# The second gate of a hybrid block as pairs of seven half-depth products, with the compressed tokens and both gates in another order

## The chip, the cores and the metric

The kernel runs on 1 core of one Trainium2 chip. The metric is the device time of one execution in microseconds. The kernel before takes 1617.92 us, the median of 3 runs (1616.51 to 1618.95).

## What is computed

One decoder block for a sequence of 1024 positions of width 1024. Two branches read the same normalized input `xn`: a gated linear recurrence (branch a) and a sparse attention over compressed, selected and window tokens (branch b). A sigmoid gate per channel weighs each branch before they are added:

```python
proj = xn @ w_in[l]
a_q, a_f, a_i, a_g, b_q, b_kv, b_gate, m_gate = jnp.split(proj, SPLIT_POINTS, axis=-1)
kc, vc, ks_, vs_, kw_, vw_ = jnp.split(b_kv, 6, axis=-1)
y_a = hgrn2_mixer(a_q, a_f, a_i, a_g, lb_all[l], hgrn_norm_g[l])
y_b = nsa_mixer(b_q, kc, vc, ks_, vs_, kw_, vw_, b_gate, positions, ...)
g_a, g_b = jnp.split(jax.nn.sigmoid(m_gate), 2, axis=-1)
merged = g_a * (y_a @ w_br_a[l]) + g_b * (y_b @ w_br_b[l])
h = h + merged @ w_out[l]
hn = rmsnorm(h, norm2_g[l])
h = h + jnp.square(jax.nn.relu(hn @ w_ff1[l])) @ w_ff2[l]
```

`m_gate` is 2048 wide: 1024 columns for the gate of branch a, 1024 for that of branch b. In `nsa_mixer` a small network (`compress`) makes 63 compressed keys and values per group out of `kc` and `vc`.

## The kernel before, in words

All matrix products run on TensorE on split numbers: each float32 operand is a high part and a remainder, and a product is three matmuls (`mm3`, L248 to L252: high by high, high by low, low by high). A matmul here has 128 rows of weights and 512 columns. x is kept transposed in `XT[th][q]`, where `th` is one half of the positions and `q` one half of the 1024 input channels, each as a pair `xh`, `xl`.

Weights come through a stream, `W` (L124 to L165): SP loads a tile `wraw`, ScalarE casts it to the high part `whi` (L152), and the remainder `wlo` is a subtraction (L155), on VectorE for two tiles of three and on GpSimd for the third. `get` starts loads and splits some tiles ahead. A second stream `C` (L658) brings the weights of `compress`.

The part that matters here runs, before the change, in this order:

1. Queries, forget gates and values of branch a, with the heads of the recurrence in the background.
2. The first gate and branch a's output, in the order of the list `ZSEQ`: m0 m1 m2 z0 m3 z1 ... m7 z5 z6 z7. An m is one tile of 128 gate columns over all positions (`gemm_T`, 48 matmuls, into PSUM tile `gT`) with a sigmoid of three ScalarE passes (L296 to L298). A z is one tile of `y_a @ w_br_a` (24 matmuls, into `pz`); VectorE multiplies it by the gate (L621), and SP stores it to DRAM (`ma_d`). Two z share one weight tile.
3. The compressed tokens: eight products `pp` (L631 to L638).
4. The second gate: eight more tiles of `gemm_T` with sigmoid, stored to `gb_d` (L750 to L754). `compress` (L663 to L746) runs beside them, first for keys, then for values: its hidden layer is `ph`, four chunks of 12 matmuls of 256 columns (L706 to L708), each with one weight tile of `C` and one operand `fh` that ScalarE (L699) and VectorE (L700) make in 8 instructions each; then a gelu on VectorE (L713 to L720) and two small products (`pgl`, `pc`).
5. Branch b's projections, `proj_b(0)`, then attention, merge, output product, MLP. The first stage of the MLP (`f1a` to `f1d`) already works in pairs of tiles with seven products each.

Background work is Python generators: `spawn` starts one, `pump` (called inside the products) gives it a step when its own program time has come, `drain` runs it to its end at that place of the program. The tile framework then fixes one order of instructions for each engine, and each engine works its own list strictly in that order.

Below, `ph` chunk means 12 matmuls of the hidden layer. "m6" and "z4" name tiles as above. The functions are printed with the line numbers of the profile.

Of the kernel before, what the change touches and what calls it, by code (L numbers as in the profile page):

```python
# [33 lines left out]
C_AQ, C_AF, C_AI, C_AG, C_BQ, C_KV, C_BG, C_MG = 0, 512, 1024, 1536, 2048, 2560, 3328, 3352  # L34


def split_const(v, bits=12):
    parts = []
    r = v
    for _ in range(3):  # L40
        e = math.floor(math.log2(abs(r)))
        s = 2.0 ** (e - bits + 1)
        p = math.floor(r / s) * s
        parts.append(p)
        r -= p
# [9 lines left out]
def tile_hybrid_block(ctx, tc, x, positions, norm1_g, w_in, lb_param, hgrn_norm_g, pe_k, pe_v,  # L55
                      w1_k, w2_k, w1_v, w2_v, w_br_a, w_br_b, w_out, norm2_g, w_ff1, w_ff2,
                      final_g, out):
    nc = tc.nc
# [5 lines left out]
    dram = ctx.enter_context(tc.tile_pool(name="dram", bufs=1, space=bass.MemoryType.DRAM))  # L64
# [4 lines left out]
    w_in2 = w_in[0]  # L69

    def psA(name="psA"):
        return ps.tile([128, 1024], F32, name=name, tag="A", bufs=2)

    def psB(name="psB"):
        return ps.tile([128, 512], F32, name=name, tag="B", bufs=4)

    def s4(dt=F32, name="s4"):
        return sl4.tile([128, 1024], dt, name=name, tag="s4", bufs=NS4)

    def a8(name="a8"):  # L80
        return act.tile([128, 4, 512], F32R, name=name, tag="a8", bufs=8)


    bg = []
    clock = [0.0]

    def pump(ns):
        clock[0] += ns
        for e in list(bg):
            while e[1] <= clock[0]:  # L90
                try:
                    lag = next(e[0])
                except StopIteration:
                    bg.remove(e)
                    break
                e[1] = clock[0] + lag

    def spawn(gen, delay=0.0):
        e = [gen, clock[0] + delay]
        bg.append(e)  # L100
        return e

    def drain(e):
        while e in bg:
# [19 lines left out]
    class Stream:  # L124
# [5 lines left out]
        def add(self, srcs, shape):  # L130
            self.specs.append((srcs if isinstance(srcs, list) else [srcs], shape))
# [60 lines left out]
    def add_vg2(h):  # L192
        for i in range(4):
            W.add([vg_w[:, i * 2:(i + 1) * 2, e, h * 128:(h + 2) * 128] for e in range(2)], (2, 512))

    for h in range(1, 4):
# [3 lines left out]
            add_vg(h)  # L200
        elif h == 2:
            add_vg2(h)
    ZSEQ = []
    for ct in range(8):
        ZSEQ.append(("m", ct))
        if ct >= 2:
            ZSEQ.append(("z", ct - 2))
    ZSEQ += [("z", 6), ("z", 7)]
    for kind, ct in ZSEQ:
        if kind == "m":  # L210
            add_mg(ct)
        elif ct % 2 == 0:
            W.add(w_cols(w_br_a[0], ct * 128, 256, k=4), (4, 256))
    for k0, k in ((0, 3), (3, 3), (6, 2)):
        W.add([w_cols(w_in2, C_KV, 256, k0=k0, k=k), w_cols(w_in2, C_BG, 24, k0=k0, k=k)], (k, 280))
    for ct in range(8):
        add_mg(8 + ct)
# [67 lines left out]
    def gemm_T(w, o=None):  # L285
        o = o or psA("gT")
        for th in range(2):
            for kt in range(KT):
                mm3(o[:, th * 512:(th + 1) * 512], (w[0][:, kt, :], w[1][:, kt, :]), X_mov(kt, th),
                    kt == 0, kt == KT - 1)  # L290
                if kt % 4 == 3:
                    pump(2600)
        return o

    def sigmoid(dst, src, tmp):
        nc.scalar.activation(tmp, src, AF.Exp, scale=-1.0)  # L296
        nc.scalar.activation(tmp, tmp, AF.Ln, bias=1.0)
        nc.scalar.activation(dst, tmp, AF.Exp, scale=-1.0)  # L298
# [3 lines left out]
    yaT = {}  # L302
# [105 lines left out]
    P1, P2, P3, P4 = split_const(2.0 * math.pi)  # L408
# [4 lines left out]
    for which in range(2):  # L413
# [7 lines left out]
        r = trig[:, which]  # L421
# [157 lines left out]
    hg = [spawn(hgrn(0))]  # L579
# [45 lines left out]
    cos, sin = trig[:, 0], trig[:, 1]
    gat = attc.tile([128, NT, 24], F32)
# [3 lines left out]
    kct = [s4(name="kct").rearrange("p (t c) -> p t c", t=4) for _ in range(2)]  # L630
    for t in range(NT):  # L631
        p = psB("pp")
# [130 lines left out]
    def proj_b(th):  # L763
        for dst, n in ((KV, "kvt"), (QT, "qt")):
            ws = [W.get() for _ in range(4)]
            dst[th] = [s4(name=n).rearrange("p (t c) -> p t c", t=2) for _ in range(2)]
            for j in range(4):
                p = psB("pp")
                for kt in range(KT):
                    w = ws[kt // 2]  # L770
                    mm3(p, X_st(kt, th * 4 + j), (w[0][:, kt % 2, :], w[1][:, kt % 2, :]), kt == 0, kt == KT - 1)
                    if kt % 2 and kt < 7:
                        pump(1300)
                nc.scalar.copy(dst[th][j // 2][:, j % 2, :], p)
# [644 lines left out]
    for th in range(2):  # L1419
# [11 lines left out]
        for dh in range(2):  # L1431
# [54 lines left out]
    for s, (k, a, b) in enumerate(seq):  # L1486
# [6 lines left out]
        i, p = a, b  # L1493
# [50 lines left out]
```

## Time and profile before

| | |
|---|---|
| median of 3 runs | 1617.92 us (1616.51 to 1618.95) |
| the profiled execution's own time | 1621.0 us |
| its span in the profile | 1619.0 us |
| mean granted clock of TensorE | 0.997 |
| TensorE (PE) busy | 1597.3 us, 99% of the span |
| VectorE (DVE) busy | 1090.5 us, 67% |
| ScalarE (ACT) busy | 744.7 us, 46% |
| GpSimd (POOL) busy | 579.8 us, 36% |

The profiled execution took 3.1 us more than the median of the runs. The span ends 2.0 us short of its execution's own time. The engine names in the rows are PE for matmuls, PEld for loads of weights into TensorE, DVE, ACT, POOL, and SP for the queue that issues the transfers. The share of busy time is a mean over stages with different limits; the change touches the stretch from about 262 us (end of the recurrence) to about 525 us (first projection of branch b).

### The profile page before, as it was taken

The page shows a single profiled execution, that of the slowest core. Times are in us where ns is not written, and L with a number is a line of the kernel's source. Part 1 is how long each engine was busy: PE and PEld are TensorE (multiplying, and loading weights), DVE is VectorE, ACT ScalarE, POOL GpSimd, SP SyncE. Part 2 cuts the span into 40 slices and gives each one's busy share as a digit, 9 for nine tenths or more (in the row PEclk, how much of TensorE's full clock was granted, in tenths as well). Part 3 has the DMA queues.
Part 4 walks back from the last instruction along what each step waited for, and adds up shares of the span by engine and source line. Part 5 has one row for each costly group of instructions (what it writes and reads, how often), then busy time and mean ns, then how long its engine had stood idle before and what let it go on. Part 6 is the DMA issues. An engine that isn't in the chain of part 4 may idle for free.

```text
span 1619.0 us, 22567 instructions
## 1 busy us (share of the span) xinstructions
PE 1597.3 (99%) x8150; PEld 1331.3 (82%) x8150; DVE 1090.5 (67%) x1635; ACT 744.7 (46%) x1430; POOL 579.8 (36%) x567
## 2 busy tenths in 40 slices
PE   8999999999999999999999999999999999999998
PEld 7898888889888888788878887888888888888886
DVE  5554444122537466988887567888999868888766
ACT  4344244230646365877774324433333445334443
POOL 2122122010112364434341124455665302654454
PEclk9999999999999999999999999999999999999999
DMA  6201011232425000000028742344444599988752
GB/s 190 73 27 53 21 45 27 89 109 79 134 91 172 27 1 1 1 1 1 1 66 286 264 139 78 134 153 144 150 143 152 205 345 315 324 302 312 281 187 104
DMA packets 143777, 211.64 MB, mean 131 GB/s; under 512 B 11649, under 2 KB 70193, under 8 KB 143666
## 3 DMA queue, kind: packets, MB, share of 16 engines
q1 hardware_dynamic: 143666, 210.21, 38.7%
q8 instruction: 64, 1.05, 0.3%
q14 instruction: 47, 0.39, 0.1%
HBM read 164.03 MB, written 46.14 MB: 130 GB/s over the span
## 4 chain that ended last, share of the span: by engine, by line
PE 89%; DVE 4%; ACT 3%; issue 1%; DMA 1%; SPq 1%; POOL 0%; POOLq 0%; DVEq 0%; ACTq 0%
PE f1c L1268 8%; PE f1d L1268 5%; PE gT L251 5%; PE gT L249 5%; PE gT L250 5%; PE f1a L1268 5%; PE oT L1087 4%; PE sc L936 4%; PE pT L976 4%; PE gA L250 3%; PE gA L249 3%; PE gA L251 3%; PE gB L249 3%; PE gB L250 3%; PE gB L251 3%; PE pp L249 2%
## 5 line engine op out<-in xcount | busy, mean ns | idle before, releaser
L1356 POOL TENSOR_TENSOR gr<-gw 128x512 f32<-128x512 f32 x80 | 123.7, 1558 | 135.0 <-DMA gw<-in_w_ff_dram 74.4
L155 POOL TENSOR_TENSOR wlo<-wraw,whi 128x1024 fp32r<-128x1024 f32 (+1 forms) x28 | 67.8, 2420 | 278.0 <-ACT whi L152 272.5
L249 PE MATMUL gT<-xh,whi 128*128 128x512 f32 x384 | 152.5, 397 | 0.0
L251 PE MATMUL gT<-xh,wlo 128*128 128x512 f32 x384 | 150.0, 391 | 0.0
L250 PE MATMUL gT<-xl,whi 128*128 128x512 f32 x384 | 149.8, 390 | 0.0
L155 DVE TENSOR_TENSOR wlo<-wraw,whi 128x1024 fp32r<-128x1024 f32 (+2 forms) x59 | 81.9, 1394 | 96.7 <-ACT whi L152 92.2
L961 POOL TENSOR_SCALAR P<-P,den,gat 128x640 f32<-128x640 f32 (+7 forms) x128 | 100.1, 797 | 120.6 <-DVE den L957 61.1
L1237 DVE TENSOR_TENSOR gu<-gr,gu 128x512 fp32r<-128x512 f32 x112 | 109.8, 981 | 48.2 <-ACT gu L1236 48.1
L1236 ACT CAST gu<-gr 128x512 fp32r<-128x512 f32 x112 | 69.4, 620 | 139.6 <-DVE gx L1237 105.4
L1268 PE MATMUL f1c<-xoh,w1op 128*128 128x512 f32 x384 | 126.1, 390 | 0.0
L979 DVE TENSOR_TENSOR pth<-pT,pth 128x512 fp32r<-128x512 f32 (+1 forms) x148 | 98.8, 683 | 21.5 <-ACT pth L978 20.0
L952 ACT ACTIVATE P<-sc,den 128x640 f32<-128x640 f32 (+7 forms) x128 | 89.7, 705 | 44.0 <-DVE den L943 40.8
L1237 DVE TENSOR_TENSOR gx<-gr,gx 128x512 fp32r<-128x512 f32 x112 | 102.5, 915 | 2.9 <-ACT gx L1236 2.8
L936 PE MATMUL sc<-kS,qS 128*128 128x512 f32 (+3 forms) x384 | 96.7, 361 | 0.8 <-ACT P L952 0.8
L1087 PE MATMUL oT<-pth,vS 128*128 128x512 f32 x264 | 96.7, 441 | 0.0
L978 ACT CAST pth<-pT 128x512 fp32r<-128x512 f32 (+1 forms) x148 | 85.1, 588 | 24.3 <-PE pT L976 21.4
L943 DVE TENSOR_REDUCE den<-sc 128x1 f32<-128x640 f32 (+7 forms) x96 | 84.6, 884 | 16.7 <-PE sc L939 16.1
L152 ACT CAST whi<-wraw 128x1024 fp32r<-128x1024 f32 (+2 forms) x87 | 88.5, 1038 | 12.0 <-PE po L250 6.1
L250 PE MATMUL gA<-gx,gu 128*128 128x512 f32 x224 | 87.4, 390 | 0.4 <-DVE gx L1237 0.2
L249 PE MATMUL gA<-gx,gu 128*128 128x512 f32 x224 | 87.3, 390 | 0.0
L251 PE MATMUL gA<-gx,gu 128*128 128x512 f32 x224 | 87.2, 389 | 0.0
L250 PE MATMUL gB<-gx,gu 128*128 128x512 f32 x224 | 87.1, 389 | 0.0
(345 smaller groups left out, 4394.5 us busy)
## 6 DMA issues: line engine op xcount, KB each, us to landing
gw<-in_w_ff_dram SPq DMA_DIRECT2D x160, 256.0 KB, 5.3
gr<-u_d SPq DMA_DIRECT2D x112, 256.0 KB, 4.8
wraw<-in_w_in_dram SPq DMA_DIRECT2D x40, 512.0 KB, 5.1
w1r<-in_w_ff_dram SPq DMA_DIRECT2D x32, 512.0 KB, 4.4
wraw<-in_w_out_dram SPq DMA_DIRECT2D x16, 512.0 KB, 6.9
u_d<-ua SPq DMA_DIRECT2D x16, 512.0 KB, 2.8
u_d<-ub SPq DMA_DIRECT2D x16, 512.0 KB, 2.8
u_d<-uc SPq DMA_DIRECT2D x16, 512.0 KB, 2.8
```

The lines of the kernel that those rows point to most:

```text
L155: eng.tensor_tensor(lo, raw, fb(hi), op=OP.subtract)
L249: nc.tensor.matmul(o, l[0], r[0], start=start, stop=False)
L250: nc.tensor.matmul(o, l[0], r[1], start=False, stop=False)
L251: nc.tensor.matmul(o, l[1], r[0], start=False, stop=stop)
L936: nc.tensor.matmul(sc[:, cs], qS[th][g][:, hh, qsl], kS[half][br][:, g * 2 + x_, ks], start=x_ == 0, stop=x_ == 1 and not masks)
L952: nc.scalar.activation(PP[qb, g, i], sv[:, hh - h0], AF.Exp, bias=den[:, 2, i:i + 1], accum_out=den[:, 0, i:i + 1])
L961: nc.gpsimd.tensor_scalar(pv_, pv_, den[:, 1, i:i + 1], gat[:, qb, (g * 4 + h_) * 3 + 1 + br:(g * 4 + h_) * 3 + 2 + br], op0=OP.mult, op1= ...
L979: nc.vector.tensor_tensor(pth[:n, 1], pt[:n], fb(pth[:n, 0]), op=OP.subtract)
L1087: nc.tensor.matmul(oT, vv, pth[:m, x_], start=i == 0 and x_ == 0, stop=i == n - 1 and x_ == 1)
L1237: nc.vector.tensor_tensor(l, src, fb(h), op=OP.subtract)
L1268: nc.tensor.matmul(dst, w_[:, kt, :], x_.kt(kt), start=first and kt == 0 and i == 0, stop=kt == 3 and i == 2, skip_group_check=True)
L1356: nc.gpsimd.tensor_tensor(t0[:, 1], t1[:, 0], t1[:, 1], op=OP.add if GORDER[i][1][2] > 0 else OP.subtract)
```

## The change

The order of the program's stages becomes: compressed tokens (`pp`) first, then m0 m1 z0 m2 z1 m3 z2 m4 z3 m5 m6 m7 z4 z5 z6 z7, then the second gate. `compress` is spawned after m0 and drained at m5. Line numbers below are those of the kernel after.

The second gate is no longer eight tiles of 48 matmuls. Two neighbouring tiles (256 columns) are a pair, and the 2 by 2 blocks of a pair (two halves of the input channels, two halves of the positions by two column tiles) are multiplied with seven products of 12 matmuls (`P1` to `P7`) in place of eight. The seven need sums of blocks of x and of weights:

- `factors()` (L743 to L761) makes S1, S2 and S4 from `XT`, in two halves, each as a high and a low part of 128x1024. For each half GpSimd adds twice (L748, L749); VectorE has one more addition (L751), four additions and subtractions (L754, L755, L758, L759) and three remainders (L738); ScalarE has three casts (L737). It is spawned when m5 has been written into the program, and drained at m7.
- `factor3()` (L763 to L774) stores the x block `XT[1][0]` to DRAM (`xs_d`) and puts S3 in its place: for each half one GpSimd instruction (L771), two on VectorE (L772, L773), a cast and a remainder. It runs in steps beside z4 to z7. The block is loaded back after the gate (L928).
- For each pair `gate_load` fetches two tiles of 512 KB, `gate_sums` makes four sums of 128x512 on GpSimd (L795), `gate_prep` splits each of seven operands (ScalarE L807, VectorE L808), and `gate_prod` runs the 12 matmuls (L830) and the additions of the results on VectorE and ScalarE.

The weights stream is cut at the gate (`n_q`), and opened again in the last pair, for branch b's projections.

```diff
-    ZSEQ = []
-    for ct in range(8):
-        ZSEQ.append(("m", ct))
-        if ct >= 2:
-            ZSEQ.append(("z", ct - 2))
-    ZSEQ += [("z", 6), ("z", 7)]
+    for k0, k in ((0, 3), (3, 3), (6, 2)):
+        W.add([w_cols(w_in2, C_KV, 256, k0=k0, k=k), w_cols(w_in2, C_BG, 24, k0=k0, k=k)], (k, 280))
+    ZSEQ = [("m", 0), ("m", 1)]
+    for ct in range(4):
+        ZSEQ += [("z", ct), ("m", ct + 2)]
+    ZSEQ += [("m", 6), ("m", 7)] + [("z", ct) for ct in range(4, 8)]
...
-    cmp_ = spawn(compress())
-    for ct in range(8):
-        pg = gemm_T(W.get())
-        gb = s4(name="gb")
-        sigmoid(gb, pg, gb)
-        nc.sync.dma_start(gb_d[ct * 128:(ct + 1) * 128, :], gb)
...
+    def split_f(nm, i, v):
+        h, l = both(nm, i)
+        nc.scalar.copy(h, v)
+        nc.vector.tensor_tensor(l, v, fb(h), op=OP.subtract)
...
+    def factors():
+        for i in range(2):
+            (h11, l11), (h12, l12), (h21, l21), (h22, l22) = [[fb(x_) for x_ in both(nm, i)]
+                                                              for nm in ("A11", "A12", "S3", "A22")]
+            s1, s2 = ftile(), ftile()
+            nc.gpsimd.tensor_tensor(s1, h21, h22, op=OP.add)
+            nc.gpsimd.tensor_tensor(s2, l21, l22, op=OP.add)
+            yield 4000.0
+            nc.vector.tensor_tensor(s1, s1, s2, op=OP.add)
+            split_f("S1", i, s1)
+            yield 2600.0
+            nc.vector.tensor_tensor(s2, s1, h11, op=OP.subtract)
+            nc.vector.tensor_tensor(s2, s2, l11, op=OP.subtract)
+            split_f("S2", i, s2)
+            yield 4000.0
+            nc.vector.tensor_tensor(s1, h12, s2, op=OP.subtract)
+            nc.vector.tensor_tensor(s1, s1, l12, op=OP.add)
+            split_f("S4", i, s1)
+            yield 4000.0
...
+            nc.gpsimd.tensor_tensor(s1, h11, h21, op=OP.subtract)
+            nc.vector.tensor_tensor(s2, l11, l21, op=OP.subtract)
+            nc.vector.tensor_tensor(s1, s1, s2, op=OP.add)
+            split_f("S3", i, s1)
...
+        sub(ta[:, 0], b12, b11)
+        sub(ta[:, 1], b22, ta[:, 0])
+        sub(tb[:, 0], b22, b12)
+        sub(tb[:, 1], b21, ta[:, 1])
...
+        for kt in range(4):
+            xh, xl = [x_[:, kt % 2, :] for x_ in both(G_X[nm], kt // 2)]
+            for i, (w_, x_) in enumerate(((h, xh), (h, xl), (l, xh))):
+                nc.tensor.matmul(dst, w_[:, kt, :], x_, start=first and kt == 0 and i == 0,
+                                 stop=kt == 3 and i == 2, skip_group_check=True)
...
+            if ct == 0:
+                cmp_ = spawn(compress())
+                W.load, W.ahead = 2, 1
+            elif ct == 1:
+                for e in hg:
+                    drain(e)
+            elif ct == 5:
+                drain(cmp_)
+                fac = spawn(factors())
+            elif ct == 7:
+                drain(fac)
+                spawn(factor3())
...
+    for s, (p, nm) in enumerate(g_seq):
+        if s == 0:
+            gate_sums(0)
+            gate_load(1)
+        while n_gp < min(len(g_seq), s + 4):
+            gate_prep(*g_seq[n_gp])
+            n_gp += 1
...
+        gate_prod(p, nm)
...
     proj_b(0)
-    drain(cmp_)
```

The change moves instructions on every engine. Two places show what follows from it. The first is VectorE's list between the middle and the end of the z tiles. Before, it holds products of a gate with a z (L621) and remainders of weights (L155) and nothing else:

```order
L621 TENSOR_TENSOR ga<-ga,pz 128x1024 x2
L155 TENSOR_TENSOR wlo<-wraw,whi 128x1024 x2
L621 TENSOR_TENSOR ga<-ga,pz 128x1024 x2
L155 TENSOR_TENSOR wlo<-wraw,whi 128x1024
L155 TENSOR_TENSOR wlo<-wraw,whi 128x840
L621 TENSOR_TENSOR ga<-ga,pz 128x1024
L155 TENSOR_TENSOR wlo<-wraw,whi 128x560
L155 TENSOR_TENSOR wlo<-wraw,whi 128x1024
L621 TENSOR_TENSOR ga<-ga,pz 128x1024 x3
```

In the kernel after, the same engine's list from the second half of `factors()` on, where the two L901 are the products of z4 and z5 and the last row is the remainder of the weights of z6 and z7 (`ft` are sums in the making, `xf` the parts of S1, S2 and S4):

```order
L738 TENSOR_TENSOR xf<-ft,xf 128x1024
L751 TENSOR_TENSOR ft<-ft 128x1024
L754 TENSOR_TENSOR ft<-ft,xh 128x1024
L901 TENSOR_TENSOR ga<-ga,pz 128x1024
L738 TENSOR_TENSOR xf<-ft,xf 128x1024
L755 TENSOR_TENSOR ft<-ft,xl 128x1024
L758 TENSOR_TENSOR ft<-xh,ft 128x1024
L738 TENSOR_TENSOR xf<-ft,xf 128x1024
L759 TENSOR_TENSOR ft<-ft,xl 128x1024
L901 TENSOR_TENSOR ga<-ga,pz 128x1024
L738 TENSOR_TENSOR xf<-ft,xf 128x1024
L155 TENSOR_TENSOR wlo<-wraw,whi 128x1024
```

The sums of x now stand in the list between the last remainder of m7's weights and the one that z6 needs.

The second place is GpSimd's list. Before, from the last head of the recurrence to the projections of branch b, it is remainders of weights and the copies of tokens of `compress` (L675):

```order
L155 TENSOR_TENSOR wlo<-wraw,whi 128x1024
L675 TENSOR_SCALAR tok<-kct 128x8x64 x4
L155 TENSOR_TENSOR wlo<-wraw,whi 128x1024 x3
L675 TENSOR_SCALAR tok<-kct 128x8x64 x4
L155 TENSOR_TENSOR wlo<-wraw,whi 128x1024 x5
```

After, the four remainders are followed by the additions of `factors()` and `factor3()`. The first L155 that stands alone is that of `ph` chunk 1 of the values, the second that of z4's and z5's weights:

```order
L155 TENSOR_TENSOR wlo<-wraw,whi 128x1024 x3
L648 TENSOR_SCALAR tok<-kct 128x8x64 x4
L155 TENSOR_TENSOR wlo<-wraw,whi 128x1024
L748 TENSOR_TENSOR ft<-xh 128x1024
L749 TENSOR_TENSOR ft<-xl 128x1024
L155 TENSOR_TENSOR wlo<-wraw,whi 128x1024
L748 TENSOR_TENSOR ft<-xh 128x1024
L749 TENSOR_TENSOR ft<-xl 128x1024
L771 TENSOR_TENSOR ft<-xh 128x1024 x2
```

GpSimd has six additions of 128x1024 in the stretch in which VectorE makes the sums.

## Rows read from the trace of the kernel before

**Rows 1.** The page's first part (busy time) and fourth part (chain that ended last).
```profile
PE 1597.3 (99%) x8150; PEld 1331.3 (82%) x8150; DVE 1090.5 (67%) x1635; ACT 744.7 (46%) x1430; POOL 579.8 (36%) x567
...
PE 89%; DVE 4%; ACT 3%; issue 1%; DMA 1%; SPq 1%; POOL 0%; POOLq 0%; DVEq 0%; ACTq 0%
```

**Rows 2.** Windows: stretch and length, busy PE, PEld, DVE, ACT, POOL, clock, DMA.
```profile
480.00:500.00 20.00, 20.00 (x102) 17.04 (x101) 13.85 (x25) 19.16 (x34) 5.34 (x3) 1.00 0.43 145
500.00:525.00 25.00, 24.52 (x124) 20.08 (x123) 16.69 (x28) 13.01 (x26) 5.41 (x3) 1.00 0.51 159
...
1018.00:1094.00 76.00, 76.00 (x339) 62.81 (x338) 66.28 (x77) 28.73 (x49) 36.74 (x25) 1.00 0.45 153
```

**Rows 3.** TensorE's waits from 262 to 545 us: total, times, longest.
```profile
PE py L570 <- DVE h L564: 1.0, 1, 1.0
PE ph L249 <- ACT whi L152: 0.5, 1, 0.5
```

**Rows 4.** TensorE's timeline: start, duration, instruction; first matmuls of three tiles in a row.
```profile
294.49 0.39 PE L249 MATMUL gT<-xh,whi 128*128 128x512 f32 x1
...
305.37 0.39 PE L249 MATMUL pz<-yah,whi 128*128 128x512 f32 x1
...
310.81 0.39 PE L249 MATMUL gT<-xh,whi 128*128 128x512 f32 x1
```

**Rows 5.** The chain that ended last, 1020 to 1040 us (the MLP's seven products).
```profile
1028.93 2.72 PE f1d L1268 x12
```

**Rows 6.** VectorE's timeline, single instructions.
```profile
272.31 1.23 DVE L155 TENSOR_TENSOR wlo<-wraw,whi 128x1024 fp32r<-128x1024 f32 x1
...
281.76 1.22 DVE L621 TENSOR_TENSOR ga<-ga,pz 128x1024 f32<-128x1024 f32 x1 [0.82 <-PE pz L251]
...
513.51 1.75 DVE L719 RECIPROCAL ct<-ct 126x256 f32<-126x256 f32 x1
515.30 0.43 DVE L720 TENSOR_TENSOR ct<-ct 126x256 f32<-126x256 f32 x1
```

**Rows 7.** ScalarE's timeline, 487 to 497 us.
```profile
487.86 2.47 ACT L699 ACTIVATE fh<-tokS,cols 128x63 fp32r<-128x63 f32 x8
490.23 1.04 ACT L152 CAST whi<-wraw 128x1024 fp32r<-128x1024 f32 x1
```

**Rows 8.** VectorE and GpSimd at the same time, 487 to 497 us (two timelines, one view).
```profile
487.99 2.63 DVE L155 TENSOR_TENSOR wlo<-wraw,whi 128x1024 fp32r<-128x1024 f32 x1 [1.63 <-ACT whi L152]
...
487.14 2.40 POOL L155 TENSOR_TENSOR wlo<-wraw,whi 128x1024 fp32r<-128x1024 f32 x1 [22.68 <-ACT whi L152]
491.35 2.45 POOL L155 TENSOR_TENSOR wlo<-wraw,whi 128x1024 fp32r<-128x1024 f32 x1 [1.80 <-ACT whi L152]
...
L700 DVE SCALAR_TENSOR_TENSOR fh<-tokS,cols,fh x16: 301/307/2395, 490.6 to 496.1; 128x63 fp32r<-128x63 f32 x16
```

**Rows 9.** Both engines again, from 263 us, in the last head of the recurrence.
```profile
263.51 1.37 DVE L503 TENSOR_TENSOR h<-qT,h 128x512 f32<-128x512 f32 x1 [0.53 <-ACT h L502]
264.81 1.78 DVE L506 TENSOR_TENSOR h<-h,h 128x512 f32<-128x512 f32 x1
...
263.04 1.30 POOL L508 TENSOR_TENSOR h<-h,vg 128x512 f32<-128x512 f32 x1 [3.26 <-ACT h L298]
264.42 1.62 POOL L509 TENSOR_TENSOR h<-h,hng 128x512 f32<-128x512 f32 x1
```

**Rows 10.** The page's sixth part (transfers): queue, count, KB each, us to landing.
```profile
wraw<-in_w_in_dram SPq DMA_DIRECT2D x40, 512.0 KB, 5.1
```

**Rows 11.** A long idle time of TensorE, and the clock after it (windows of 1 us).
```profile
995.66 0.65 PE L1150 MATMUL pt<-ident,hn 128*128 128x128 f32 x4 [2.52 <-DVE xol L1156]
...
996.00:997.00 1.00, 1.00 (x7) 0.86 (x6) 1.00 (x3) 0.59 (x1) 0.72 (x1) 0.91 0.00 0
997.00:998.00 1.00, 1.00 (x7) 0.80 (x5) 1.00 (x1) 0.00 (x0) 1.00 (x2) 0.50 0.00 0
...
1000.00:1001.00 1.00, 1.00 (x7) 0.78 (x6) 0.40 (x1) 0.25 (x1) 1.00 (x2) 0.89 0.00 0
```

More of the change, by code (lines that the diff above doesn't have):

```diff
@@ L746, in compress, with both @@
             yield 500.0
-    cmp_ = spawn(compress())
-    for ct in range(8):
-        pg = gemm_T(W.get())
-        gb = s4(name="gb")
-        sigmoid(gb, pg, gb)
-        nc.sync.dma_start(gb_d[ct * 128:(ct + 1) * 128, :], gb)
-        if ct == 6:
-            W.load, W.ahead = 5, 4
+    XF = {"A11": XT[0][0], "A12": XT[0][1], "A22": XT[1][1], "S3": XT[1][0]}
+    xs_d = dram.tile([2, 128, 4, 512], F32, name="xs_d")
+    def both(nm, i):
+        if nm in ("S1", "S2", "S4"):
+            if nm not in XF:
+                XF[nm] = tuple([s4(F32R, name="xf").rearrange("p (a c) -> p a c", a=2) for _ in range(2)]
+                               for _ in range(2))
+            return [x_[i] for x_ in XF[nm]]
+        return [x_[:, 2 * i:2 * i + 2, :] for x_ in XF[nm]]
@@ new lines, in gate_prep @@
+    def gate_prep(p, nm):
+        if nm == G_ORDER[3] and p + 1 < GPAIRS:
+            gate_sums(p + 1)
+        op = s4(F32R, name="gwo")
+        h, l = [op[:, x_ * 512:(x_ + 1) * 512].rearrange("p (a c) -> p a c", a=4) for x_ in range(2)]
+        nc.scalar.copy(h, GWS[p][G_W[nm]])
+        nc.vector.tensor_tensor(l, GWS[p][G_W[nm]], fb(h), op=OP.subtract)
+        G_OP[p, nm] = (h, l)
+        if nm == G_ORDER[-1]:
+            del GWS[p], GWR[p]
+            if p + 2 < GPAIRS:
+                gate_load(p + 2)
@@ new lines, in gate_prod, with gate_out @@
+    def gate_prod(p, nm):
+        if nm == "P1":
+            G_PS[p] = {"a": psB("ga")}
+        elif nm == "P6":
+            pa = psA("gc")
+            G_PS[p].update(c=pa[:, :512], e=pa[:, 512:])
+        elif nm == "P7":
+            G_PS[p]["d"] = psB("gd")
+        ps_ = G_PS[p]
+        dst = ps_[{"P1": "a", "P2": "a", "P6": "c", "P7": "d", "P4": "d", "P5": "e", "P3": "e"}[nm]]
+        first = nm in ("P1", "P6", "P7", "P5")
+        h, l = G_OP.pop((p, nm))
+        for kt in range(4):
[3 more added lines that the diff above has]
+                                 stop=kt == 3 and i == 2, skip_group_check=True)
+            if kt == 1:
+                pump(1300)
+        pump(1300)
+        add = lambda o, a, b: nc.vector.tensor_tensor(o, a, b, op=OP.add)
+        neg = lambda o, a: nc.scalar.activation(o, a, AF.Exp, scale=-1.0)
+        def gate_out(ct, g):
+            nc.scalar.activation(g, g, AF.Ln, bias=1.0)
+            nc.scalar.activation(g, g, AF.Exp, scale=-1.0)
+            nc.sync.dma_start(gb_d[ct * 128:(ct + 1) * 128, :], g)
+        if nm == "P1":
+            G_T[p] = [s4(name="gp"), s4(name="gu")]
+            nc.scalar.copy(G_T[p][0][:, :512], ps_["a"])
+        elif nm == "P6":
+            add(G_T[p][0][:, 512:], ps_["c"], G_T[p][0][:, :512])
+        elif nm == "P7":
+            add(G_T[p][1][:, :512], ps_["d"], G_T[p][0][:, 512:])
+        elif nm == "P2":
+            G_G[p] = [s4(name="gb") for _ in range(2)]
+            neg(G_G[p][0][:, :512], ps_["a"])
+        elif nm == "P5":
+            g = G_G[p][1][:, 512:]
+            add(g, ps_["e"], G_T[p][1][:, :512])
+            neg(g, g)
+        elif nm == "P4":
+            g = G_G[p][0][:, 512:]
+            add(g, ps_["d"], G_T[p][0][:, 512:])
+            neg(g, g)
+            gate_out(2 * p, G_G[p][0])
+        else:
+            g = G_G[p][1][:, :512]
+            add(g, ps_["e"], G_T[p][0][:, 512:])
+            neg(g, g)
+            gate_out(2 * p + 1, G_G[p][1])
+            del G_G[p], G_T[p], G_PS[p]
@@ new lines, in tile_hybrid_block @@
+    GA = {}
+    for kind, ct in ZSEQ:
+        if kind == "m":
+            pg = gemm_T(W.get())
+            GA[ct] = s4(name="ga")
+            sigmoid(GA[ct], pg, GA[ct])
+            if ct == 0:
[10 more added lines that the diff above has]
+                spawn(factor3())
+            continue
+        if ct % 2 == 0:
+            wa = W.get()
+        if ct == 6:
+            gate_load(0)
+        pz = psA("pz")
+        cs = slice((ct % 2) * 128, (ct % 2) * 128 + 128)
+        for th in range(2):
+            ts_ = slice(th * 512, (th + 1) * 512)
+            for kt in range(4):
+                mm3(pz[:, ts_], (wa[0][:, kt, cs], wa[1][:, kt, cs]),
+                    (yaT[kt][0][:, ts_], yaT[kt][1][:, ts_]), kt == 0, kt == 3)
+            pump(2600)
+        nc.vector.tensor_tensor(GA[ct], GA[ct], pz, op=OP.mult)
+        nc.sync.dma_start(ma_d[ct * 128:(ct + 1) * 128, :], GA.pop(ct))
@@ new lines, in tile_hybrid_block @@
+    for e in list(bg):
+        drain(e)
+    yaT.clear()
+    wa = None
+    g_seq = [(p, nm) for p in range(GPAIRS) for nm in G_ORDER]
+    n_gp = 0
+    for s, (p, nm) in enumerate(g_seq):
[5 more added lines that the diff above has]
+            n_gp += 1
+        if s == len(g_seq) - 7:
+            W.stop = n_before_merge
+            W.load, W.ahead = 5, 4
+            W.ensure(W.i + 4, W.i)
+        elif s == len(g_seq) - 3:
+            W.ensure(W.i + 4, W.i + 2)
+        gate_prod(p, nm)
@@ L760, in tile_hybrid_block @@
+    for nm in ("S1", "S2", "S4"):
+        del XF[nm]
+    for x_ in range(2):
+        nc.sync.dma_start(fb(XF["S3"][x_]), xs_d[x_])
     KV, QT = {}, {}
@@ L883, in tile_hybrid_block @@
     proj_b(0)
-    drain(cmp_)
-    kct = None
     W.load, W.ahead = 4, 3
```

55 lines of the change are left out of this document (30 added, 25 removed).

## The prediction, made before the changed kernel ran

> **What bounds the kernel now.** I began with the page's busy times and chain of waits: TensorE is busy 99% of the span and holds 89% of the chain [rows 1]. So removed matmuls are time, if everything that TensorE reads is still ready. Next came the windows of the stretch that the change touches: from 480 to 500 us TensorE is full at clock 1.00, while VectorE works 13.85 of 20 us, and ScalarE, which then makes `compress`'s operands beside a sigmoid, 19.16 of 20 [rows 2]. Then TensorE's waits: from 262 to 545 us it waits 1.5 us in all [rows 3]. The stretch has no idle time to win, and a TensorE with that little slack shows every operand that comes late. Last I followed the order of each engine's list after the change, with durations from the timelines.
>
> **Matmuls removed.** A tile of 48 matmuls takes 305.37 − 294.49 = 10.88 us and a z of 24 takes 5.44 [rows 4]: 0.227 us each, 2.72 us for 12, and the MLP's groups of 12 matmuls show the same 2.72 us [rows 5]. Eight tiles are 32 groups of 12; four pairs of seven are 28. The gain is 4 × 2.72 = **10.9 us**. The 0.5 us that `compress`'s tail costs in `proj_b(0)` [rows 2, 3] goes too, since that tail is over long before. Together **−11.4 us**.
>
> **The gate stage itself: nothing.** The MLP's first stage has the same groups of seven and runs with TensorE at 76.00 of 76 us although VectorE is busy 66.28 and GpSimd 36.74 [rows 2]. A pair of gate tiles has on VectorE seven remainders and five additions of 128x512: 12 of some 0.9 us, 11 of 19 us. Four sums on GpSimd at 1.3 to 1.6 us [rows 9] are at most 6.4 us. If the first products wait for their sums, it is by about 1 us at most; I keep that for the upper end. The two weight tiles of a pair land in 5.1 us each [rows 10], against 19 us for a pair. The block that is loaded back is first read after the 24 or so groups of `proj_b(0)`. The compressed tokens and the first gate are moved with all their instructions, transfers included, and not changed: nothing. The last head of the recurrence, for which TensorE waited 1.0 us before [rows 3], now ends beside other products: between 1 us less and 1 us more, as the row says no more than its size; I take 0.
>
> **What is added between m5 and z6.** VectorE's instruction of 128x1024 takes 1.23 us, its product of a gate with z 1.22, the reciprocal in the gelu 1.75 [rows 6]; GpSimd's takes 2.40 [rows 8]; eight operands `fh` on ScalarE 2.47, a cast 1.04 [rows 7]. I walked the lists with these, from 0 at the last matmul of m5.
>
> How VectorE and GpSimd share is the question on which the sum turns. A remainder on VectorE that met one on GpSimd, begun 0.85 us before it, took 2.63 us where it takes 1.23 alone; one `fh` of 16, 307 ns at the median, took 2395 while GpSimd worked 2.45 us [rows 8]. GpSimd's own 2.40 does not grow when it came first. In the recurrence the two alternate, one instruction each, and both get longer [rows 9]. So I count each GpSimd instruction as a turn in which VectorE stands, if VectorE's reads two tiles from SBUF, as every sum and remainder here does. The Trainium skill says the same on its page "SBUF — State Buffer", section "Who interferes with whom": VectorE and GpSimd share one pair of ports under an exclusive lock, and the one that issued first keeps it for the whole instruction; by it the change comes out slower by the 14 us of the sum below, without it 0.3 us slower.
>
> *In m6.* `compress` is drained in m5, so chunks 1 to 3 of the values' `ph` fall among m6's 48 matmuls. ScalarE does m5's sigmoid, eight `fh` and the cast for chunk 1 by 6.3; GpSimd's remainder lasts to 8.7, and the first two additions of `factors()` stand right behind it. VectorE's eight `fh` of chunk 2 get one in after each of them (to 11.35, to 14.0), the other six after; then chunk 2's remainder is done at 16.7 and, after eight more `fh`, chunk 3's at 19.85. TensorE waits 1.8 for chunk 1, 4.85 for chunk 2, 0.25 for chunk 3: **6.9 us**; m6 ends at 23.2, not 16.3. With no turns it would be 1.9.
>
> *From m7 to z6.* VectorE's remainder for m7 runs from 22.85 to 24.1. Up to the end of the remainder that z6 needs there follow 17 instructions of 1.23 (20.9), two products of z4 and z5 (2.4) and the rest of the gelu (3.5): 26.8 us, so 50.9 with VectorE never waiting. TensorE would be there at about 46, after m7, z4 and z5 and two matmuls that need only the high part. That alone is 4.9 us short. GpSimd's five instructions in between (z4's weights, two additions, two of S3) are five turns of 2.4, of which some 1.3 us fall where VectorE waits anyway: 50.9 + 12.0 − 1.3 = 61.6. TensorE loses 61.6 − 46.0 = **15.6 us**: about 0.9 in m7, 2.7 before z4 (its remainder on GpSimd waits for a cast that stands behind the last of `compress` on ScalarE), 12 before z6. Without turns it would be 0.9 + 1.8 + 5.4 = 8.1.
>
> *Clock.* A wait of 2.52 us in the MLP was followed by a granted clock of 0.91, then three windows at 0.50 (1.2 of 2.4 GHz), then 0.89 [rows 11]: 0.09 + 1.5 + 0.11 = 1.7 us of work lost. The waits for chunk 2 and before z6 are both longer. The first is followed by shorter waits that hide some of it: 1.5 + 1.7 = **3.2 us**.
>
> **Sum.** −11.4 + 6.9 + 15.6 + 3.2 = +14.3 us. The profiled execution took 1621.0 us, 3.1 above the median; the sum on it is 1635, on the median of 1617.9 **1632 us**, which I give.
>
> **Rivals.**
>
> *The turns are not taken* (no change). If VectorE keeps going while its next instruction stands ready, only its own 26.8 us count: 1.9 in m6, 8.1 to z6, one fall of the clock 1.7, less 11.4: +0.3, 1618 us. For it: most of VectorE's instructions here follow each other at once, so GpSimd may get in more seldom. Against: the `fh` in rows 8 did follow each other at once, and one was held 2.4 us all the same.
>
> *VectorE is not behind* (faster). The point that decides is TensorE's whole idle time from m6 to z6 under 8 us. GpSimd or the scheduler's order would have to let the sums of the first half run in m6, where VectorE waits for ScalarE's `fh`; then at z6 about 2 to 3 us are missing and the gain stays: −11.4 + 2 = 1608 to 1609 us. For it: over 480 to 500 us VectorE is 31% idle [rows 2]. Against: its list is worked in order, and the first sum stands behind m7's remainder.
>
> *The gate stage runs late* (slower still). If its operands come late in each pair, as VectorE (11 us) and GpSimd take turns, by 2 us a pair: 4 × 2 = 8 more, 1640 us. Against: the MLP's stage, with more work per pair, doesn't wait [rows 2].
>
> *The change doesn't do what it says*: the lists hold 48 matmuls of 128x512 fewer and all the sums; I give it no chance of its own.
>
> **How the numbers follow.** The forecast, with both waits, has 0.68 and spans by itself 1624 (z6 short by 4 to 5 us less, no fall of the clock after m6) to 1638 (1 for the recurrence, 1 for the first pair, 1.7 for one more fall of the clock, 2 for the walk). No change has 0.11, faster 0.14, slower still 0.07. A measurement of this kernel tells about 0.2%, 3.2 us, from no change. From 1613 to 1638 leaves out the faster case and most of the late gate, 0.2. Faster 0.14, same 0.11, slower 0.75.
>
> **What would show it.** In the changed profile: TensorE's list of waits has `ph` on VectorE's remainder or on its `fh` with some 5 us, and `pz` of z6 on VectorE's L155 with about 12 us, the longest wait of the stretch; windows of 1 us behind it show the clock at 0.50; VectorE's sums L751 to L759 take over 2 us where GpSimd's L748, L749 and L771 run and 1.23 elsewhere; the gate's groups of 12 follow at 2.72 us, and the stage of four pairs takes 76 us. Wrong: an idle time before z6 under 5 us; sums at 1.23 beside GpSimd's; waits inside the gate's pairs of more than 1 us; or a loss elsewhere in the stretch, above all in the first compressed tokens and m0 to m5, where I counted none.

## The result, and the profile after

The changed kernel takes 1635.6 us, the median of its runs, against 1617.92 before: a ratio of 1.0111, 95% interval 1.0096 to 1.0126. Timed a second time beside the experiments it took 1634.99 against 1618.45, ratio 1.0099 (1.0084 to 1.0114). It is slower, by 16 to 18 us; 14.3 were forecast (1632 us). The first profiled execution of the changed kernel ran at a mean granted clock of 0.83 (1810.95 us), so the profile shown here is that of its second timing: span 1633.0 us, own time 1634.79 us, clock 0.993.

Busy times, the page's first part; they answer to the first of [rows 1]. TensorE's 48 matmuls fewer are there (8102 for 8150), and its share is 97% where it was 99%:

```profile
PE 1590.4 (97%) x8102; PEld 1324.0 (81%) x8102; DVE 1158.9 (71%) x1700; ACT 763.9 (47%) x1470; POOL 615.7 (38%) x586
```

The window of the gate stage (same columns as [rows 2]): TensorE is busy all 76.00 us, and the four pairs take 28 × 2.72 = 76.2:

```profile
434.00:510.00 76.00, 76.00 (x337) 62.80 (x336) 41.27 (x51) 41.27 (x62) 20.60 (x13) 1.00 0.44 159
```

TensorE's waits from 205 to 525 us, in place of the two of [rows 3]:

```profile
PE pz L246 <- ACT whi L152: 10.1, 1, 10.1
PE ph L247 <- DVE wlo L155: 3.5, 1, 3.5
PE pp L246 <- ACT gat L611: 2.3, 1, 2.3
PE pz L248 <- POOL wlo L155: 1.8, 1, 1.8
PE ph L247 <- POOL wlo L155: 1.2, 1, 1.2
PE py L567 <- DVE h L561: 0.6, 1, 0.6
PE ph L246 <- ACT whi L152: 0.4, 1, 0.4
PE gT L248 <- DVE wlo L155: 0.3, 1, 0.3
```

20.2 us, where there were 1.5. The first is z6: its first matmul waits for ScalarE's cast, which stands behind the last cast of the sums in ScalarE's list, and that one waits for VectorE:

```profile
421.27 0.79 PE L246 MATMUL pz<-yah,whi 128*128 128x512 f32 x1 [10.09 <-ACT whi L152]
...
419.23 1.04 ACT L737 CAST xf<-ft 128x1024 fp32r<-128x1024 f32 x1 [2.49 <-DVE ft L759]
420.18 1.04 ACT L152 CAST whi<-wraw 128x1024 fp32r<-128x1024 f32 x1
```

VectorE's timeline up to that place shows why (start, duration, instruction, idle time before it and what ended it):

```profile
370.42 5.91 DVE L673 SCALAR_TENSOR_TENSOR fh<-tokS,cols,fh 128x63 fp32r<-128x63 f32 x7
376.25 1.21 DVE L155 TENSOR_TENSOR wlo<-wraw,whi 128x1024 fp32r<-128x1024 f32 x1
377.38 1.90 DVE L673 SCALAR_TENSOR_TENSOR fh<-tokS,cols,fh 128x63 fp32r<-128x63 f32 x8
...
385.17 1.22 DVE L155 TENSOR_TENSOR wlo<-wraw,whi 128x1024 fp32r<-128x1024 f32 x1
...
399.38 2.11 DVE L738 TENSOR_TENSOR xf<-ft,xf 128x1024 fp32r<-128x1024 f32 x1 [1.21 <-ACT xf L737]
406.14 3.40 DVE L751 TENSOR_TENSOR ft<-ft 128x1024 f32<-128x1024 f32 x1 [4.65 <-POOL ft L749]
...
411.86 2.67 DVE L738 TENSOR_TENSOR xf<-ft,xf 128x1024 fp32r<-128x1024 f32 x1
...
421.45 1.22 DVE L155 TENSOR_TENSOR wlo<-wraw,whi 128x1024 fp32r<-128x1024 f32 x1
```

GpSimd's timeline over the same time:

```profile
370.36 2.42 POOL L748 TENSOR_TENSOR ft<-xh 128x1024 f32<-128x1024 f32 x1
372.71 2.40 POOL L749 TENSOR_TENSOR ft<-xl 128x1024 f32<-128x1024 f32 x1
397.54 2.87 POOL L155 TENSOR_TENSOR wlo<-wraw,whi 128x1024 fp32r<-128x1024 f32 x1 [22.42 <-ACT whi L152]
400.37 3.38 POOL L748 TENSOR_TENSOR ft<-xh 128x1024 f32<-128x1024 f32 x1
403.72 2.40 POOL L749 TENSOR_TENSOR ft<-xl 128x1024 f32<-128x1024 f32 x1
406.07 2.40 POOL L771 TENSOR_TENSOR ft<-xh 128x1024 f32<-128x1024 f32 x1
```

Seven `fh` take 5.91 us while two additions run on GpSimd, the eight of the next chunk 1.90, and the remainder that TensorE waits 3.5 us for in m6 stands behind the seven. From the remainder for m7 (to 386.39) to that for z6 (to 422.67) VectorE needs 36.3 us. At 406.07 the two engines meet: GpSimd's addition begins 0.07 us before VectorE's, takes its usual 2.40, and VectorE's takes 3.40. The Trainium skill says on the page "SBUF — State Buffer", section "Who interferes with whom", that issue order decides who blocks; this pair of rows agrees.

The clock in the windows around z6: none of the 5 us is worked in the first, the second is at 0.50, which is 1.2 GHz:

```profile
415.00:420.00 5.00, 0.00 (x0) 0.00 (x0) 4.96 (x5) 1.81 (x2) 0.00 (x0) 0.50 0.00 0
420.00:425.00 5.00, 3.73 (x8) 2.65 (x9) 5.00 (x6) 1.22 (x2) 0.00 (x0) 0.50 0.77 248
```

### The profile page after: what moved, and what is told of

It is laid out like the page before. It is cut to its first block, busy times and chain, and to the rows that moved or that the text cites. A ratio compares the mean times of both kernels' runs of the same rounds, so it can differ in the third digit from the quotient of the medians.

```text
span 1809.2 us, 22647 instructions
## 1 busy us (share of the span) xinstructions
PE 1774.0 (98%) x8102; PEld 1388.5 (77%) x8102; DVE 1137.9 (63%) x1700; ACT 768.5 (42%) x1470; POOL 588.3 (33%) x586
## 4 chain that ended last, share of the span: by engine, by line
PE 92%; DVE 2%; issue 2%; SPq 1%; ACT 1%; POOL 1%; DMA 1%; POOLq 0%; ACTq 0%
PE f1c L1438 8%; PE f1d L1438 5%; PE f1a L1438 5%; PE oT L1257 4%; PE sc L1106 4%; PE pT L1146 4%; PE gT L246 3%; PE gT L247 3%; PE gT L248 3%; PE gA L246 3%; PE gA L248 3%; PE gA L247 3%; PE gB L246 3%; PE gB L248 3%; PE gB L247 3%; PE pp L246 2%
## 5 line engine op out<-in xcount | busy, mean ns | idle before, releaser
L1526 POOL TENSOR_TENSOR gr<-gw 128x512 f32<-128x512 f32 x80 | 117.7, 1476 | 160.5 <-DVE gu L1407 58.5
L1407 DVE TENSOR_TENSOR gu<-gr,gu 128x512 fp32r<-128x512 f32 x112 | 119.9, 1071 | 52.8 <-ACT gu L1406 52.7
L155 POOL TENSOR_TENSOR wlo<-wraw,whi 128x1024 fp32r<-128x1024 f32 (+1 forms) x25 | 61.7, 2468 | 271.1 <-ACT whi L152 236.5
L1438 PE MATMUL f1c<-xoh,w1op 128*128 128x512 f32 x384 | 136.5, 418 | 0.0
L155 DVE TENSOR_TENSOR wlo<-wraw,whi 128x1024 fp32r<-128x1024 f32 (+2 forms) x54 | 78.9, 1472 | 83.5 <-ACT whi L152 83.5
L246 PE MATMUL gT<-xh,whi 128*128 128x512 f32 x256 | 116.1, 454 | 0.0
L247 PE MATMUL gT<-xl,whi 128*128 128x512 f32 x256 | 113.9, 445 | 0.0
L248 PE MATMUL gT<-xh,wlo 128*128 128x512 f32 x256 | 113.1, 442 | 0.1
L1106 PE MATMUL sc<-kS,qS 128*128 128x512 f32 (+3 forms) x384 | 101.9, 376 | 0.5 <-ACT P L1122 0.5
L246 PE MATMUL gB<-gx,gu 128*128 128x512 f32 x224 | 93.7, 418 | 0.0
L246 PE MATMUL gA<-gx,gu 128*128 128x512 f32 x224 | 93.7, 418 | 0.0
L248 PE MATMUL gA<-gx,gu 128*128 128x512 f32 x224 | 93.3, 417 | 0.0
L248 PE MATMUL gB<-gx,gu 128*128 128x512 f32 x224 | 93.3, 417 | 0.0
L247 PE MATMUL gB<-gx,gu 128*128 128x512 f32 x224 | 93.0, 415 | 0.0
```

The costliest lines, as they stand in the source:

```text
L155: eng.tensor_tensor(lo, raw, fb(hi), op=OP.subtract)
L1106: nc.tensor.matmul(sc[:, cs], qS[th][g][:, hh, qsl], kS[half][br][:, g * 2 + x_, ks], start=x_ == 0, stop=x_ == 1 and not masks)
L1407: nc.vector.tensor_tensor(l, src, fb(h), op=OP.subtract)
L1438: nc.tensor.matmul(dst, w_[:, kt, :], x_.kt(kt), start=first and kt == 0 and i == 0, stop=kt == 3 and i == 2, skip_group_check=True)
L1526: nc.gpsimd.tensor_tensor(t0[:, 1], t1[:, 0], t1[:, 1], op=OP.add if GORDER[i][1][2] > 0 else OP.subtract)
```

## The experiments

The kernel before was timed beside each group of runs: 1618.45 us beside the changed kernel again, the run without GpSimd's additions, the first one without any sums of x and the steps of `compress`; 1617.60 beside the counter, the copies on ScalarE, the sums on VectorE and all repairs together; 1618.27 beside the others. Where a run is compared with the changed kernel of another group, the difference is also given as counted from the kernel before.

**The changed kernel again.**

> The changed kernel once more, unaltered, for a profile at full clock. The theory (operands late in m6 and before z6, because VectorE's sums of x and GpSimd's additions take turns): about 1635 us; TensorE idle some 5 to 7 us in m6 for ph, some 15 us from m7 to z6, of which about 12 before z6; the four pairs of the gate take 76 us without a wait. If instead the gate stage were slow: waits of over 1 us inside its pairs and a stage of over 80 us, with less idle time before z6.

1634.99 us; its rows are those above. The gate stage runs without a wait; 5.1 us of waits for `ph` in m6, 12.2 us from m7 to z6 (0.3, 1.8, 10.1). The places are the expected ones; m6 lies in its range, z6 is 1.9 us smaller than expected and the way from m7 to z6 2.8.

**Without GpSimd's additions.**

```diff
-            nc.gpsimd.tensor_tensor(s1, h21, h22, op=OP.add)
-            nc.gpsimd.tensor_tensor(s2, l21, l22, op=OP.add)
...
-            nc.vector.tensor_tensor(s1, s1, s2, op=OP.add)
+            nc.vector.tensor_tensor(s1, h21, h22, op=OP.add)
...
-            nc.gpsimd.tensor_tensor(s1, h11, h21, op=OP.subtract)
...
-            nc.vector.tensor_tensor(s1, s1, s2, op=OP.add)
+            nc.vector.tensor_tensor(s1, h11, s2, op=OP.add)
```

> Leaves out GpSimd's six additions of 128x1024 for the sums of x; VectorE keeps its count of instructions and reads the blocks of x themselves, so S1 and S3 miss parts of the sums. Theory of turns (VectorE stands while GpSimd works on two tiles in SBUF): the waits in m6 fall from 6.9 to 2 us, those from m7 to z6 from 15.6 to about 8, the whole is 12 to 14 us faster than the changed kernel, about 1622 us, and VectorE's instructions of 128x1024 there take 1.23 us. Rival (only the length of VectorE's own list counts): within 2 us of the changed kernel, about 1635 us.

1621.8 us, 13.2 less than the changed kernel: the expectation of the turns, and far from that of length alone. TensorE's waits there:

```profile
PE pz L246 <- ACT whi L152: 2.8, 1, 2.8
...
PE ph L247 <- POOL wlo L155: 1.2, 1, 1.2
```

The 3.5 us for `ph` on VectorE are gone, z6 waits 2.8 and not 10.1. VectorE's list has its full length. The eight `fh` of the chunk in question, in the changed kernel and then here:

```profile
368.28 8.04 DVE L673 SCALAR_TENSOR_TENSOR fh<-tokS,cols,fh 128x63 fp32r<-128x63 f32 x8 [0.91 <-ACT fh L672]
...
368.55 3.84 DVE L673 SCALAR_TENSOR_TENSOR fh<-tokS,cols,fh 128x63 fp32r<-128x63 f32 x8 [0.92 <-ACT fh L672]
```

One remainder on GpSimd runs beside them in both, the two additions only in the first, so the turns in m6 are shown. From m7 to z6 this run does not split how much was VectorE held during a GpSimd instruction and how much was VectorE idle until GpSimd's sum was there: the rows above show both, three held instructions (0.9 + 2.2 + 1.4 us over 1.23) and one idle time of 4.65.

**Without any sums of x.** The factors and their store and reload are left out, with `G_X` pointing at blocks of x:

```diff
-    G_X = {"P1": "A11", "P2": "A12", "P3": "S4", "P4": "A22", "P5": "S1", "P6": "S2", "P7": "S3"}
+    G_X = {"P1": "A11", "P2": "A12", "P3": "A12", "P4": "A22", "P5": "A22", "P6": "A11", "P7": "S3"}
...
-                fac = spawn(factors())
...
-                drain(fac)
-                spawn(factor3())
```

> Leaves out all sums of x (factors and factor3, the store and reload of the block): the gate's seven products read blocks of x in their place. Everything else of the change stays. Theory: only the gain of 10.9 + 0.5 us and some 2 to 3 us of waits for ph in m6 remain, 1608 to 1610 us. Rival (the gate stage or the other order itself costs): 1615 us or more.

1616.85 us, ratio to before 0.9987 (0.9977 to 0.9996). This is a miss: 7 us of the gain are still gone with all sums left out, so something outside the sums costs. The traces name two places. The first stands in the changed kernel's waits above, `pp` on `gat`, with the clock below 1.00 behind it. VectorE's timeline there, in the changed kernel:

```profile
229.94 2.38 DVE L490 TENSOR_TENSOR_SCAN h<-scan,h 128x512 f32<-128x512 f32 x1
...
235.34 1.75 DVE L503 TENSOR_TENSOR h<-h,h 128x512 f32<-128x512 f32 x1
237.02 0.41 DVE L610 COPY kct<-pp 128x256 f32<-128x256 f32 x1
```

The copy of the first `pp`, a product begun at 225.4, stands behind a scan and products of the last recurrence head, so the fourth product (the expectation further down calls it the fifth) finds no PSUM buffer. The second place is the merge, some 340 us after the gate. TensorE's waits from 835 to 900 us, in the kernel before:

```profile
PE pz L249 <- ACT whi L152: 0.4, 1, 0.4
```

and in the changed kernel, which does not touch that code:

```profile
PE pz L248 <- POOL wlo L155: 2.7, 2, 1.4
PE pT L1146 <- DVE pth L1149: 0.5, 1, 0.5
PE pz L246 <- ACT whi L152: 0.4, 1, 0.4
```

Two remainders for which TensorE waits are on GpSimd now. The stream counts its tiles and gives every third to GpSimd; eight gate tiles no longer pass through it.

**The counter.**

```diff
             W.stop = n_before_merge
+            W.k += 8
             W.load, W.ahead = 5, 4
```

> In the changed kernel the stream's counter, by which every third remainder goes to GpSimd, is raised by 8 where the stream is opened again after the gate, so that from there on the same tiles go to GpSimd as in the kernel before. Theory (eight tiles fewer in the stream have moved the slow remainders onto tiles for which TensorE then waits, in the merge): TensorE's two waits of 1.4 us for a remainder on GpSimd in the merge, and the shorter ones there, go; 3 us faster than the changed kernel, about 1632 us. Rival (those waits come from the loads or from the later start): no difference.

1631.55 us, 3.4 less than the changed kernel as it stands and 2.6 less counted from the kernel before. TensorE's waits from 830 to 990 us are those of the kernel before again:

```profile
PE pz L246 <- ACT whi L152: 0.4, 1, 0.4
```

**The copies of the compressed tokens on ScalarE.**

```diff
-        nc.vector.tensor_copy(kct[t // 4][:, t % 4, :], p[:, :256])
+        nc.scalar.copy(kct[t // 4][:, t % 4, :], p[:, :256])
```

> In the changed kernel the copies of the compressed tokens out of PSUM (L610) are on ScalarE in place of VectorE. Theory (the compressed tokens now run while VectorE works off the last head of the recurrence, its first copy stands behind a scan and two products there, and the fifth product waits for that PSUM buffer): the wait of 2.3 us at the fifth product and the fall of the clock behind it go, 2 to 3.5 us faster, about 1632 us. Rival (ScalarE itself is behind by as much): no difference.

1631.84 us, 3.1 less as it stands and 2.3 less counted from the kernel before; the row `pp` on `gat` is gone, the others stay. The intervals of this run and of the counter's (1.0069 to 1.0104 and 1.0069 to 1.0100) overlap that of the changed kernel, so what shows the two causes is the waits that went, and the next run, which has both edits.

**The gate without sums, with both repairs.** The two edits above on the kernel without any sums of x.

> As no_x_sums (leaves out all sums of x, so the seven products read blocks of x in their place), with the two repairs that were measured since: the counter raised after the gate and the copies of the compressed tokens on ScalarE. Theory (the terms add up: 1616.9 less 3.4 less 3.1, and what stays are some 3 us of waits for ph and its gelu): 1609 to 1612 us. If the seven products cost more than 28 groups of 2.72 us: 1613 us or more.

1608.18 us, ratio 0.9939 (0.9919 to 0.9960), 10.1 us less than before, where the kernel without the two edits was 1.6 less; that is 0.8 us under the expected range. The gate's 28 groups take 76.2 us again, so the seven products give their 10.9 us, and 4.0 us of idle time stay in the stretch.

**Steps of `compress`.**

```diff
-                yield 3000.0
+                yield 2600.0
```

> One change to the changed kernel: the five steps of compress's hidden layer are 2600 ns of program time apart, not 3000, so that all ph chunks of the values stand in m5 and none in m6, and the rest of the gelu is done before the sums. Theory: the waits in m6 go (7 us and a fall of the clock), the sums start some 20 us earlier, and before z6 5 to 7 us of idle time stay: 1635 - 8 - 9 = 1616 to 1620 us. Theory of length alone: no wait before z6 at all, 1608 to 1611 us. If the waits in m6 had another cause than the chunks: within 3 us of the changed kernel.

1627.85 us, 7.1 less than the changed kernel and 8 to 12 above what was expected. TensorE's waits:

```profile
PE pz L246 <- DVE ga L901: 4.8, 1, 4.8
PE ph L247 <- DVE wlo L155: 3.9, 1, 3.9
```

The chunks stand in m5 as meant, but GpSimd's first two additions moved up with them: they start at 357.70 and 360.17, in the middle of eight `fh` that take 6.08 us, and the wait of 3.5 is there again as 3.9. z6, which begins at 409.43, waits only 1.0 and 0.7 us, less than the 5 to 7 expected. The longest wait has moved to z7 and to another resource: TensorE waits for the PSUM buffer that z5's product with its gate frees, and that product (L901, at 419.65) stands behind the sums for S3 in VectorE's list. That wait was in no theory.

**Sums of x on VectorE.**

```diff
-            nc.gpsimd.tensor_tensor(s1, h21, h22, op=OP.add)
-            nc.gpsimd.tensor_tensor(s2, l21, l22, op=OP.add)
+            nc.vector.tensor_tensor(s1, h21, h22, op=OP.add)
+            nc.vector.tensor_tensor(s2, l21, l22, op=OP.add)
...
-            nc.gpsimd.tensor_tensor(s1, h11, h21, op=OP.subtract)
+            nc.vector.tensor_tensor(s1, h11, h21, op=OP.subtract)
```

> In the changed kernel GpSimd's six additions of the sums of x are on VectorE. Theory of turns (an addition of 2.4 us on GpSimd holds VectorE for 2.4, the same addition on VectorE takes 1.23): although VectorE gets 7.4 us more work, m6 loses some 3.5 us of waits and z6 waits no longer than now; 4 to 8 us faster than the changed kernel, 1627 to 1631 us. Theory of length alone: 5 to 7 us slower, 1640 us or more.

1635.07 us, as the changed kernel (0.9 more counted from the kernel before): both theories miss. The waits moved:

```profile
PE pz L246 <- ACT whi L152: 6.2, 2, 4.8
PE ga L830 <- ACT gwo L807: 2.7, 1, 2.7
...
PE pz L248 <- POOL wlo L155: 2.0, 1, 2.0
PE ga L830 <- DVE gwo L808: 1.5, 1, 1.5
```

m6 lost its 3.5 us and z6 waits 4.8, as the turns would have it; but VectorE's longer list ends later, and the gate's first product waits 4.2 us for operands that stand behind S3. Four of the instructions for S3 take 2.31 us each there, beside GpSimd's sums for the gate, so turns have a part in this wait too. From 200 to 540 us, idle time plus work lost to the clock (in windows of 1 us) is 17.2 + 7.4 = 24.6 us, against 20.1 + 5.0 = 25.1 in the changed kernel. The six additions cost TensorE about the same on either engine here.

**All repairs together.** The counter, the copies on ScalarE, the sums on VectorE, 2600 in place of 3000 in `compress` and of 4000 in `factors()`, and:

```diff
-                eng = nc.gpsimd if self.k % 3 == 0 else nc.vector
+                eng = nc.gpsimd if self.k % self.third == 0 else nc.vector
...
             if ct == 0:
                 cmp_ = spawn(compress())
                 W.load, W.ahead = 2, 1
+                W.third = C.third = 10 ** 6
...
             elif ct == 5:
                 drain(cmp_)
+                W.load, W.ahead = 3, 2
...
             W.stop = n_before_merge
+            W.k += 8
+            W.third = 3
```

> All repairs together: the counter raised after the gate, copies of the compressed tokens on ScalarE, sums of x on VectorE, every remainder from m1 to the gate on VectorE, steps of compress's hidden layer and of factors 2600 ns apart, and z6's weights split one tile earlier. Theory: of the waits some 2 to 4 us stay at the gate's first product, where VectorE's list is 42 us long against 44 us of TensorE's work; 1607 to 1612 us, faster than the kernel before by 6 to 11 us. If the seven-product stage had a cost of its own, it would stay above 1613 us.

1612.23 us, ratio 0.9967 (0.9954 to 0.9980), 0.2 above the upper end of what was expected. The waits that stay are again those at the end of VectorE's list:

```profile
PE pz L246 <- DVE ga L903: 3.8, 2, 2.5
PE ga L830 <- DVE gwo L808: 1.2, 1, 1.2
```

**Sums begun earlier.** Three versions on top of it. All spawn `factors()` one or two tiles before m5's end and put the product of a gate with z ahead of the next step; they differ in the tile and in the steps (2600 after m4; 5200 after m3; 5200 after m4). The last one's difference from the combined version, without its longer steps:

```diff
+            elif ct == 4:
+                fac = spawn(factors())
             elif ct == 5:
                 drain(cmp_)
                 W.load, W.ahead = 3, 2
-                fac = spawn(factors())
...
-            pump(2600)
+            if th == 0:
+                pump(2600)
         nc.vector.tensor_tensor(GA[ct], GA[ct], pz, op=OP.mult)
+        pump(2600)
```

> As combined, but the sums of x are spawned after m4, not m5, one tile earlier, and the product of a gate with z stands ahead of the next step of the sums on VectorE. Theory (VectorE's list between m6 and the gate was the bound, and had idle time in m4 and m5): the two waits of TensorE for z's PSUM buffer (3.8 us) and that at the gate's first product (1.2 us) go; in return the sums share VectorE with the fh of compress in m5, and up to 3 us of waits for ph come there. 1606 to 1611 us.

1610.75 us; the waits before the gate are gone, 3.0 us of waits for `gT` came at 379 to 382 us, where m7 begins, for its weights behind the sums: a return of the size named, at another tile than named.

> As sums_from_m4, but spawned after m3 and with 5200 ns between steps, so that VectorE has about half of each step free for compress. Theory: fewer waits for ph than with sums_from_m4, none before the gate: 1605 to 1609 us. If slots of the 128x1024 ring are short so early (twelve are held from then on), loads come late: 1612 us or more.

1608.05 us; one wait of 1.0 us for `gT`, for a cast on ScalarE.

> As sums_from_m4, with 5200 ns between steps as in sums_from_m3, so that the second half of the sums falls into m6 and m7. Theory: between the two others, 1606 to 1610 us; waits for ph smaller than in sums_from_m4, waits before the gate up to 2 us.

**1606.62 us**, the median of 1604.73, 1605.59, 1607.64 and one execution of 5612.39 us that nothing here explains; ratio of the other three 0.9925 (0.9902 to 0.9947): 11.7 us less than before and 28 less than the changed kernel, with the full computation. All of TensorE's waits from 205 to 600 us:

```profile
PE py L567 <- DVE h L561: 0.6, 1, 0.6
PE ph L246 <- ACT whi L152: 0.4, 1, 0.4
PE ph L247 <- DVE wlo L155: 0.2, 1, 0.2
```

The intervals of this version and of the one after m3 overlap, so which of the two is better is open.

## Why the prediction was right, and where its sum was not

The direction, the two places and the cause, GpSimd's additions beside VectorE's list, were right, and 1635.6 lies in the range. Term by term (forecast, then measured from the waits of the changed kernel's profile, the clock from its windows of 1 us):

| term | forecast | measured |
|---|---|---|
| 48 matmuls fewer | −10.9 | −10.9 (the stage takes 76.0 us without a wait) |
| old waits of the stretch | −0.5 | −0.9 (1.5 before, 0.6 of the recurrence stay) |
| waits for `ph` in m6 | +6.9 | +5.1 |
| m7 to z6 | +15.6 | +12.2 |
| clock after both | +3.2 | +3.5 |
| compressed tokens beside the recurrence, with the clock | 0 | +3.8 |
| remainders on GpSimd in the merge | 0 | +3.2 |
| sum | +14.3 | +16.0 |

The measured time moved by 16.5 to 17.7 us; between the two spans it is 14.0, as the profile of before has 1.7 us of lost clock and 1.1 us of idle time in its first 200 us that this one has not. So the sum came out near by luck, two errors against each other: 4.9 us too much in the three terms of the waits and their clock, 7.0 us not seen.

**Turns.** The walk gave VectorE five turns of 2.4 less 1.3 in m7 to z6, that is 10.7 us over its own 26.8. Measured are 36.3 − 26.8 = 9.5. But the share that was named was wrong: of held instructions the rows show about 4.5 us, and 4.65 are one idle time, VectorE waiting for the result of GpSimd's additions, which themselves came late behind z4's remainder. (Two shorter idle times, 1.21 and 0.73, are nearly made up for by neighbouring rows that overlap.) The run without those additions shows that they cause the loss (13.2 us); in m6 it shows the turns, from m7 to z6 not which of the two ways. Of the rivals the one without turns is excluded by it: 1618 was its time, 1625 with the 7.0 us that it did not see either, and the changed kernel gets near it only without GpSimd's work. The sign named for z6 came in another form: TensorE waits 10.1 us for the cast on ScalarE, and not some 12 for VectorE's remainder behind it.

**Place by place:** in m6 the wait for chunk 2 is 3.5 where 4.85 was given, and the rest agrees to 0.3 us; m7, z4 and z6 wait 0.3, 1.8 and 10.1 us where 0.9, 2.7 and 12 were given.

**"moved with all their instructions, transfers included, and not changed: nothing"** is the step that failed. The compressed tokens were costed by their own work, and not by what stands ahead of their copies on VectorE at the new place. The stream's counter was not looked at, although the remainder's engine depends on the count of tiles ahead of it. Both are shown by their runs: each edit takes its waits away, 2.3 us and 3.2 us, and without the sums of x the two together are worth 8.5 us. The late gate stage did not happen, and the faster rival needed what the last versions do: sums that begin before m6.

## What to carry to other kernels

Fewer matmuls are a gain only if the engine that makes their operands finishes earlier as well: lay its whole list between two fixed points beside TensorE's work there, 26.8 us against 22 here, before counting the gain. When the list is too long, another engine for the same sums did nothing (1635.07 against 1634.99); an earlier start, while that engine had idle time, was worth 6.3 us over the other repairs (11.7 against 5.4 us less than the kernel before). A stage that is only moved has to be costed by the queues at its new place, and a round-robin counter carries the effect of a removed tile to code hundreds of microseconds later.

## What was not expected of the hardware

After the wait of 10.1 us at z6, the windows show TensorE at 0.50 of its clock for about 3.7 us of work, a loss of 1.9 us; in windows of 1 us, the wait of 3.5 us in m6 cost 1.6, and the wait of 2.3 us in the compressed tokens 1.5 in the changed kernel and 1.7 in the kernel without sums of x. The wait's length hardly shows in these losses. A wait of 2.6 us in the MLP, at the place of [rows 11], cost nothing in the run with the copies on ScalarE. And GpSimd's addition, not only VectorE's, can be the one that is held: 3.38 us at 400.37 where its usual is 2.40, while VectorE worked at an instruction begun earlier.
